# A sliding-window attention layer: probabilities rearranged through DRAM, half 1 normalized early, finishing and low parts moved

## The chip, the cores and the metric

The kernel runs on one core of a Trainium2 chip. The metric is the device time of one execution in microseconds (us); the lower, the better. The engines named below are TensorE (PE for matmuls, PEld for its weight loads), VectorE (DVE), ScalarE (ACT), GpSimd (POOL) and SyncE (SP), which here issues all the DMA transfers.

## The reference

With DEPTH = 1 only the first mixer runs: sliding-window attention with 32 query heads of 64, 4 key/value heads, a window of 128, ALiBi penalties and one learned sink per head. All of it is float32, on 1024 tokens of 2048 features.

```python
h = rmsnorm(x, g_pre)
q, k, v, z = split(h @ w_in)              # 2048, 256, 256 and 2048 columns
for each block n of 128 queries:          # keys: blocks n-1 and n
    scores = q @ k.T / 8 - slope[head] * dist          # masked to 0 <= dist < 128
    p = softmax(concat(scores, sink[head]))[..., :-1]
    o = p @ v
y = (o * silu(z)) @ w_out
out = x + rmsnorm(y, g_post)
```

## The kernel before

**Precision.** Every float32 operand of the large products is split in a high part, rounded to the matmul's type, and a low part, the remainder. Three products (high by high, low by high, high by low) are accumulated, so each product costs three matmuls of 128 x 512. ACT makes the high part by a cast, DVE the low part by a subtraction.

**Order.** The 1024 tokens are worked in two halves of 512 (four blocks of 128). Each half has, in this order: the V projection (`v_slot`, `v_evac`), the K projection (`k_phase`, `k_evac`), the attention stage `in_phase` (called in0 and in1 here) and the output stage (out0 and out1), four chunks `c` of 512 output columns. In out0 the input of half 1 is also prepared. The fourth chunk of out1 runs block by block at the very end (`acc_l`, L793), from weights kept whole in `wl`.

**The weight stream.** `stream` lists all weight granules (128 x 512) in their order of use. `pump_dma` (L187) loads the raw granule on SP's queue, `pump_split` (L200) makes its two parts and `next_granule` (L222) hands them to the matmuls, with a look-ahead of 2 splits and 5 loads, four raw buffers and nine for low parts. In half 0 the low parts of the V, K and input projections are stored to DRAM (L218) and in half 1 loaded (L196) in place of DVE's subtraction. The output weights are split again in each half. Those of out1's fourth chunk are among the granules of its second and third chunk (`wl_hi`, `wl_lo`, both L213 and L215).

**The attention stage.** `in_phase` has 8 quads of 4 heads. A quad is 16 slots; each slot is one granule and 12 matmuls of the projections of q (two accumulators) and z (two). Events (`at(slot, ...)`, run by `run_events`) put the attention's instructions between the slots: `att_scores` (matmul L312, mask, minimum, exponential L368), `att_transpose` in slot TSL = 12 of a block's own count, `att_values` in slot VSL = 15. A block of 128 queries takes four slots. `att_transpose` divides the exponentials by their sum in three DVE operations (L377), transposes 32 x 32 squares on DVE (L384), moves 16 squares of 32 x 128 to their places (L389: nine copies on ACT, four on DVE, three on POOL), splits the result (L392, L393), and has POOL cut it into the parts of the two key blocks (L397, L401). `att_values` multiplies by the values (L422) and by the gate (L437). `f` and `g`, which hold the cut probabilities, have one buffer each.

**Normalization.** The scale of a token, 1/rms, is not applied to the input. It is multiplied in where the projections leave PSUM: `v_evac` (`rhalf`), `k_evac` (L295), `q_evac` (L460), `z_evac` (L473), the last three on DVE with the row `rrow`. In out0, `prep_load` and `x_square` compute the squares of half 1 from 1 MB loads `xt` (L679, L249, L252), and `chunk_load` (L685) with `chunk_split` (L693 to L695) transposes and splits its input.

**Finishing.** The rows of half 0 lie in `y_dram` after out0 (L718). `finalize` (L559 to L564) loads them and x, scales and adds on DVE and stores the result; this runs in slots 142 to 175, in out1.

**What orders the instructions.** At build time the tile framework orders each engine's instructions by a planned timeline; an instruction in `keep_in_program_order` stays in the order of the program among those pinned. From slot 125 of a half (PIN_FROM) through the first 13 output slots (SPILL) the matmuls are pinned. An engine works strictly in its order, so a wait holds up all that follows on it; that goes for SP's queue of transfers too.

## Time and profile before

| what | value |
|---|---|
| median of 3 runs | 1314.67 us (1310.45 to 1317.33) |
| the profiled execution | 1312.46 us |
| its span, first to last instruction | 1310.4 us |
| granted clock of TensorE, mean | 0.995 |
| PE busy | 1261.4 us, 96% |
| PEld busy | 1038.2 us, 79% |
| DVE busy | 1001.3 us, 76% |
| ACT busy | 807.4 us, 62% |
| POOL busy | 302.5 us, 23% |
| moved by DMA | 225.79 MB, 172 GB/s |

Busy is the time in which an engine has at least one instruction at work. Matmuls overlap, so a PE that is busy throughout is one that is fed throughout. A share over the whole span is an average over stages that differ, so the argument goes by stages. Idle time of an engine costs something only where another engine waits for it.

### The profile page before, as it was taken

To read this page: it belongs to the slowest core of one execution; us is meant where nothing else is said; L and a number is where in the kernel's file an instruction comes from. 1 tells how busy PE (TensorE), PEld (TensorE's weight loads), DVE (VectorE), ACT (ScalarE), POOL (GpSimd) and SP (SyncE) were. 2 spreads that over 40 slices of the span, in tenths; PEclk is the share of its full clock that TensorE was granted. 3 is DMA by queue.
4 is the path that set the end of the run, shared out by engine and by line. 5 is a ranking of instruction groups with operands and counts; after the bars stand their busy time and mean duration, and the time that the engine had idled before them with its cause. 6 is when DMAs were issued, how large, how long until landed. Compare 5 with 4: busy or idle time off the path is not lost. (4 is left out here: it accounts for less than half of the span.)

```text
span 1310.4 us, 20613 instructions
## 1 busy us (share of the span) xinstructions
PE 1261.4 (96%) x5889; PEld 1038.2 (79%) x5889; DVE 1001.3 (76%) x2840; ACT 807.4 (62%) x2131; POOL 302.5 (23%) x561
## 2 busy tenths in 40 slices
PE   8999999999999998999999999999999999998897
PEld 8888777787787776778898888888888887776676
DVE  5759999989989998676722478878878878966555
ACT  4537666666676676555533477767767767644441
POOL 1303233323323323000002033333333333300000
PEclk9999999999999999999999999999999999999999
DMA  8565545455454533967686665565555552288715
GB/s 290 176 194 161 161 153 163 151 173 162 132 177 153 170 105 90 242 162 180 171 249 189 182 180 170 166 177 171 168 176 171 169 161 81 78 274 271 251 56 187
DMA packets 263793, 225.79 MB, mean 172 GB/s; under 512 B 47088, under 2 KB 195072, under 8 KB 263680
## 3 DMA queue, kind: packets, MB, share of 16 engines
q1 hardware_dynamic: 263680, 224.48, 57.2%
q8 instruction: 47, 0.77, 0.3%
q14 instruction: 66, 0.54, 0.1%
HBM read 174.09 MB, written 50.33 MB: 171 GB/s over the span
## 5 line engine op out<-in xcount | busy, mean ns | idle before, releaser
L312 PE MATMUL acc_i<-h_hi,g_lo 128*128 128x512 f32 x1024 | 403.3, 394 | 4.9 <-DVE g_lo L215 4.5
L312 PE MATMUL acc_i<-h_hi,g_hi 128*128 128x512 f32 x1024 | 402.3, 393 | 3.1 <-ACT g_hi L213 2.9
L312 PE MATMUL acc_i<-h_lo,g_hi 128*128 128x512 f32 x1024 | 400.9, 392 | 0.0
L213 ACT CAST g_hi<-raw 128x512 fp32r<-128x512 f32 x400 | 245.6, 615 | 123.5 <-PE acc_i L312 34.1
L312 PEld LDWEIGHTS acc_i<-h_hi,g_hi 128*128 128x128 f32 x1024 | 192.5, 188 | 45.9 <-ACT g_hi L213 6.7
L312 PEld LDWEIGHTS acc_i<-h_hi,g_lo 128*128 128x128 f32 x1024 | 192.6, 188 | 44.9 <-DVE g_lo L215 11.7
L312 PEld LDWEIGHTS acc_i<-h_lo,g_hi 128*128 128x128 f32 x1024 | 192.7, 188 | 38.2
L389 ACT COPY px<-wt 32x128 f32<-32x128 f32 x576 | 171.2, 297 | 67.4 <-DVE wt L384 60.8
L215 DVE TENSOR_TENSOR g_lo<-raw,g_hi 128x512 fp32r<-128x512 f32 x256 | 186.2, 728 | 27.3 <-ACT g_hi L213 18.9
L368 ACT ACTIVATE t<-t,m 128x129 f32<-128x129 f32 x256 | 102.6, 401 | 107.3 <-DVE m L358 103.8
L397 POOL TENSOR_SCALAR_AFFINE_SELECT g<-f 64x512 fp32r<-64x512 f32 x112 | 90.5, 808 | 225.2 <-ACT f L392 218.8
L523 DVE TENSOR_TENSOR u_lo<-u,u_hi 128x512 fp32r<-128x512 f32 x128 | 88.9, 697 | 44.2 <-ACT u_hi L522 44.2
L522 ACT CAST u_hi<-u 128x512 fp32r<-128x512 f32 x128 | 78.6, 617 | 62.4 <-PE acc_l L793 24.5
L312 PE MATMUL acc_o<-g_lo,u_hi 128*128 128x512 f32 x256 | 101.9, 398 | 6.6 <-DVE g_lo L215 6.6
L312 PE MATMUL acc_o<-g_hi,u_lo 128*128 128x512 f32 x256 | 100.1, 395 | 0.0
L339 POOL COPY t<-nsink 128x4 f32<-128x4 f32 x64 | 18.6, 293 | 332.0 <-DVE w L377 208.4
L401 POOL TENSOR_SCALAR_AFFINE_SELECT f<-f 64x512 fp32r<-64x512 f32 x112 | 83.7, 747 | 39.9 <-DVE f L393 25.0
L358 DVE CUSTOM_DVE_ANT_0 t<-s_ps,t,nsink 128x128 f32<-128x128 f32 x256 | 87.6, 348 | 4.6
L312 PE MATMUL acc_o<-g_hi,u_hi 128*128 128x512 f32 x256 | 85.1, 397 | 3.6 <-ACT g_hi L213 2.6
L312 PE MATMUL acc_s<-g_lo,u_hi 128*128 128x512 f32 x192 | 75.7, 395 | 7.7 <-DVE g_lo L215 7.6
L312 PE MATMUL s_ps<-k_x,q 128*128 128x320 f32 x256 | 76.6, 311 | 4.3 <-DVE s_ps L356 1.5
L389 POOL COPY px<-wt 32x128 f32<-32x128 f32 x192 | 64.5, 336 | 68.4 <-DVE wt L384 58.0
(138 smaller groups left out, 2089.7 us busy)
## 6 DMA issues: line engine op xcount, KB each, us to landing
raw<-in_w_in_a SPq DMA_DIRECT2D x288, 256.0 KB, 3.3
lo<-g_lo SPq DMA_DIRECT2D x144, 256.0 KB, 2.1
g_lo<-lo SPq DMA_DIRECT2D x144, 256.0 KB, 3.0
raw<-in_w_out_a SPq DMA_DIRECT2D x128, 256.0 KB, 3.8
xt<-in_x SPq DMA_DIRECT2D x4, 1024.0 KB, 7.5
xb<-in_x SPq DMA_DIRECT2D x64, 64.0 KB, 3.7
y_dram<-yg SPq DMA_DIRECT2D x16, 256.0 KB, 3.6
fin_y<-y_dram SPq DMA_DIRECT2D x16, 256.0 KB, 5.2
```

The costliest lines, as they stand in the source:

```text
L213: nc.scalar.copy(hi, raw)
L215: nc.vector.tensor_tensor(lo, raw, hi.bitcast(F32), op=ALU.subtract)
L312: ins = nc.tensor.matmul(*args, **kw)
L339: nc.gpsimd.tensor_copy(a["t", b][:, :, :, P : P + 1], nsink[:, i : i + 1].unsqueeze(2).unsqueeze(3).broadcast_to([P, 2, 2, 1]))
L358: nc.vector.tensor_tensor_reduce(out=t[:, 0:P], in0=s3[:, 0, QTR:], in1=t[:, 0:P], scale=1.0, scalar=nsink[:, i : i + 1], op0=ALU.add, op1 ...
L368: nc.scalar.activation(t, t, AF.Exp, bias=m, scale=-1.0, accum_out=den)
L389: copy(x[qrows[3 - k], c, :], wt[qrows[c], 3 - k, :])
L397: nc.gpsimd.affine_select(out=g[dst].rearrange("p a (s i) -> p (a s) i", i=HD), in_=part.bitcast(F32), pattern=[[0, 2 * QUAD], [-1, HD]], ...
L401: nc.gpsimd.affine_select(out=part, in_=part.bitcast(F32), pattern=[[0, 2 * QUAD], [1, HD]], compare_op=ALU.is_ge, fill=0.0, base=0, chann ...
L522: nc.scalar.copy(hi_v, src)
L523: nc.vector.tensor_tensor(lo_v, src, hi_v.bitcast(F32), op=ALU.subtract)
```

## The change

- **Probabilities.** The division by the sum goes from three DVE operations to six ACT operations (`AF.Copy` with a scale per partition). For the first seven quads of a half the 16 moves become one DMA write of the 256 KB tile to DRAM (`pd`, four buffers) and four reads of 64 KB with the squares in their places. The last quad (`fast`) keeps the 16 moves. The tag `w` gets three buffers instead of two, `att_values` slot 17 instead of 15, and the copies of the values (`v_twice`) slot 14 instead of 12.
- **Half 1 normalized in its split.** The squares of half 1 are computed in in0 on ACT, pinned, from 16 loads of 256 KB (`xp`); `chunk_split` multiplies by the row `rrow1` on DVE. In half 1 `v_evac` scales by 0.5, and `k_evac`, `q_evac` and `z_evac` read PSUM with no multiplication first. `prep_load` and the squares leave out0; `xb` gets four buffers instead of two, `xtr` two instead of one, and the loads are issued three slots earlier.
- **Finishing.** `y_scale` and the 16 `finalize` pieces of half 0 run in in1, in slots 10 to 119, seven slots apart, with the DVE operation pinned and two buffers per tile instead of four shared.
- **Low parts.** Every granule's low part made in half 0 is stored, the output weights' 64 too, and in half 1 every granule has its low part loaded; for the fourth chunk directly into `wl`. The look-ahead of splits is 3 instead of 2, with four buffers for high parts instead of three and six for low parts instead of nine.

```diff
+G_BUFS = 4
+LOOK_W = 3
-LO_BUFS = 9
+LO_BUFS = 6
+SQ_SLOT, FIN_SLOT, FIN_STEP = 12, 10, 7
+W_BUFS = 3
+PD_BUFS = 4
-SSL, TSL, VSL = 8, 12, 15
+SSL, TSL, VSL = 8, 12, 17
...
             lo = None
-            if i - first in kept:
-                lo = lo_tile()
-                nc.sync.dma_start(lo.bitcast(F32), kept[i - first])
+            if key in kept:
+                lo = wl[1][:, kind, :] if isinstance(kind, int) else lo_tile()
+                nc.sync.dma_start(lo.bitcast(F32), kept[key])
...
             nc.scalar.copy(hi, raw)
-            if isinstance(kind, int) or made:
+            if lo is None:
+                lo = lo_tile()
                 nc.vector.tensor_tensor(lo, raw, hi.bitcast(F32), op=ALU.subtract)
-            if keeps(i):
-                kept[i] = dram.tile([P, 512], F32, name=f"lo{i}")
-                nc.sync.dma_start(kept[i], lo.bitcast(F32))
+                kept[key] = dram.tile([P, 512], F32, name=f"lo{i}")
+                nc.sync.dma_start(kept[key], lo.bitcast(F32))
...
-    def k_evac(pk, t):
-        k32 = gp.tile([P, 512], F32, tag="tmp", name="k32", bufs=1)
-        nc.vector.tensor_tensor(k32, pk, rrow, op=ALU.mult)
+    def k_evac(pk, t, half):
+        k32 = pk
+        if not half:
+            k32 = gp.tile([P, 512], F32, tag="tmp", name="k32", bufs=1)
+            nc.vector.tensor_tensor(k32, pk, rrow, op=ALU.mult)
...
-    def att_transpose(a, half, b):
+    def att_transpose(a, half, b, fast):
...
-        w = pool.tile([P, QUAD, 2, 2, QTR], F32, tag="w", name="w", bufs=2)
-        for e, dst, src, n in ((0, 0, QTR, 3), (0, 3, 0, 1), (1, 0, 0, 4)):
-            nc.vector.tensor_tensor(
-                w[:, dst : dst + n, :, e, :].rearrange("p g s i -> p s g i"),
-                t[:, :, e, src : src + n * QTR].rearrange("p s (g i) -> p s g i", i=QTR),
-                rec[:, :, e : e + 1].unsqueeze(3).broadcast_to([P, 2, n, QTR]),
-                op=ALU.mult,
-            )
+        w = pool.tile([P, QUAD, 2, 2, QTR], F32, tag="w", name="w", bufs=W_BUFS)
+        for s in range(2):
+            for e, dst, src, n in ((0, 0, QTR, 3), (0, 3, 0, 1), (1, 0, 0, 4)):
+                nc.scalar.activation(
+                    w[:, dst : dst + n, s, e, :],
+                    t[:, s, e, src : src + n * QTR].rearrange("p (g i) -> p g i", i=QTR),
+                    AF.Copy, scale=rec[:, s, e : e + 1],
+                )
...
+        if fast:
+            for n in range(QUAD * QUAD):
...
+        else:
+            pd = dram.tile([P, QUAD * P], F32, tag="pd", name="pd", bufs=PD_BUFS)
+            nc.sync.dma_start(pd, wt.rearrange("p g c -> p (g c)"))
+            src = pd.rearrange("(c i) (k j) -> k i c j", i=QTR, j=P)
+            for k in range(QUAD):
+                nc.sync.dma_start(x[qrows[k]], src[k])
...
+            if half:
+                nc.scalar.mul(qh, src[here], scale)
+                nc.vector.scalar_tensor_tensor(
+                    lo, src[here], scale, qh.bitcast(F32), op0=ALU.mult, op1=ALU.subtract
+                )
+            else:
+                nc.scalar.copy(qh, src[here])
+                nc.vector.tensor_tensor(lo, src[here], qh.bitcast(F32), op=ALU.subtract)
...
+        src = acc
+        if not half:
+            nc.vector.tensor_tensor(z, acc, rrow, op=ALU.mult)
+            src = z
+        nc.scalar.activation(th, src, AF.Tanh, scale=0.5)
+        nc.vector.scalar_tensor_tensor(z, th, 1.0, src, op0=ALU.add, op1=ALU.mult)
...
     def finalize(pool, b, c):
...
-        yt = pool.tile([P, 512], F32, tag="xt1", name="fin_y", bufs=4)
-        xt = pool.tile([P, 512], F32, tag="xt1", name="fin_x", bufs=4)
+        yt = pool.tile([P, 512], F32, tag="xt1", name="fin_y", bufs=2)
+        xt = pool.tile([P, 512], F32, tag="xt1", name="fin_x", bufs=2)
...
         def finish():
-            nc.vector.scalar_tensor_tensor(yt, yt, r2[:, 0, b : b + 1], xt, op0=ALU.mult, op1=ALU.add)
+            tc.keep_in_program_order(
+                nc.vector.scalar_tensor_tensor(yt, yt, r2[:, 0, b : b + 1], xt, op0=ALU.mult, op1=ALU.add)
+            )
...
+        def sq_load(b, c):
+            xp = att.tile([P, 512], F32, tag="xp", name="xp", bufs=1)
+            nc.sync.dma_start(xp, xf[HALF + b * P : HALF + (b + 1) * P, c * 512 : (c + 1) * 512])
+            at(SQ_SLOT + 6 * (4 * b + c) + 4, lambda: sq_make(xp, b, c))
+
+        def sq_make(xp, b, c):
+            xjunk = att.tile([P, 512], BF16, tag="oc", name="xjunk", bufs=1)
+            tc.keep_in_program_order(nc.scalar.activation(xjunk, xp, AF.Square, accum_out=ssx1[:, b, c : c + 1]))
+
+        for b in range(NB):
+            for c in range(4):
+                at(SQ_SLOT + 6 * (4 * b + c), lambda b=b, c=c: sq_load(b, c))
+        at(SQ_SLOT + 6 * 16 + 4, lambda: x_scales(ssx1, rcol1))
         in_phase(0, h0, u0, att)
...
-            xt = op.tile([P, HALF], F32, tag="xtr", name="xtr", bufs=1)
+            xt = op.tile([P, HALF], F32, tag="xtr", name="xtr", bufs=2)
             tc.keep_in_program_order(nc.vector.transpose(xt, xts.pop(("b", k))))
+            nc.vector.tensor_tensor(xt, xt, rrow1, op=ALU.mult)
...
-        for c in range(4):
-            s0 = OUT_SLOT + 12 * c
-            at(s0, lambda c=c: prep_load(c))
-            at(s0 + 5, lambda c=c: x_square(xts[c], c, junks))
         for k in range(KC):
-            at(OUT_SLOT + 3 * k, lambda k=k: chunk_load(k))
+            at(OUT_SLOT + max(3 * k - 3, 0), lambda k=k: chunk_load(k))
             at(OUT_SLOT + 3 + 3 * k, lambda k=k: chunk_split(k))
-        at(191, x_scales)
...
+        for b in range(NB):
+            at(2 * b, lambda b=b: y_scale(0, b))
+            for c in range(4):
+                s0 = FIN_SLOT + FIN_STEP * (4 * b + c)
+                at(s0, lambda b=b, c=c: fin_start(b, c))
+                at(s0 + 4, lambda b=b, c=c: fins.pop((b, c))())
         in_phase(1, h1, u1, att)
```

134 lines of the change are left out of this document (58 added, 76 removed).

## The prediction

> **What bounds the kernel now.** I read the busy times by stage first, because the stages have different limits. The columns are the stretch, its length, the busy time (and instructions) of PE, PEld, DVE, ACT and POOL, the granted clock, the DMA share and GB/s.
>
> ```profile
> core 0: us, PE busy (x) PEld busy (x) DVE busy (x) ACT busy (x) POOL busy (x), PEclk, DMA share, GB/s
> 60.20:474.30 414.10, 401.25 (x1811) 323.52 (x1809) 372.42 (x1156) 273.35 (x788) 119.82 (x214) 1.00 0.54 163
> 474.30:530.80 56.50, 50.45 (x225) 40.83 (x224) 48.17 (x130) 38.23 (x100) 15.29 (x23) 0.97 0.36 103
> 530.80:578.70 47.90, 44.41 (x194) 35.80 (x193) 33.38 (x58) 26.22 (x54) 0.00 (x0) 1.00 0.80 198
> 578.70:622.20 43.50, 43.50 (x194) 36.02 (x193) 31.34 (x52) 25.73 (x51) 0.00 (x0) 1.00 0.75 185
> 622.20:665.70 43.50, 43.50 (x193) 36.02 (x192) 27.72 (x49) 24.36 (x48) 1.42 (x1) 1.00 0.72 196
> 711.00:1100.40 389.40, 389.40 (x1826) 325.58 (x1825) 299.56 (x1009) 277.00 (x794) 121.72 (x241) 1.00 0.56 167
> 1100.40:1155.00 54.60, 50.37 (x226) 41.04 (x225) 47.51 (x123) 36.62 (x95) 17.67 (x26) 0.97 0.34 112
> 1155.00:1205.90 50.90, 46.02 (x194) 35.32 (x193) 33.04 (x52) 22.56 (x45) 0.00 (x0) 1.00 0.84 277
> 1205.90:1258.10 52.20, 46.73 (x193) 34.96 (x191) 32.16 (x51) 25.14 (x53) 0.00 (x0) 1.00 0.60 197
> ```
>
> PE is the bound, and the rows say where it is not fed. In1 (711 to 1100) is the model: PE busy in every microsecond. In0 (60 to 474) does the same projections and attention with 15 fewer matmuls recorded and needs 24.7 us more; its DVE is busy 372.4 of 414.1 us (90%), against 299.6 of 389.4 (77%) in in1. An output chunk that is fully fed takes 43.5 us (third and fourth chunk of out0), a slot of 12 matmuls 43.5 / 16 = 2.72 us. The second chunk of out0 is 4.4 us over that, the second and third of out1 7.4 and 8.7 us. These four sums, 24.7 + 4.4 + 7.4 + 8.7 = 45.2 us, are what the edits can reach; both first output chunks also hold the last quad's attention.
>
> The list of waits names what PE's feeders stood for (total us, times, longest):
>
> ```profile
> DVE junk L252 <- DMA xt<-in_x: 12.0, 4, 3.7
> DVE wl_lo L215 <- ACT wl_hi L213: 21.0, 9, 3.1
> DVE fin_y L563 <- DMA fin_x<-in_x: 12.9, 8, 3.0
> ACT wl_hi L213 <- DMA raw<-in_w_out_a: 46.6, 15, 5.1
> PEld o_ps L422 <- POOL f L401: 11.0, 16, 1.9
> PE o_ps L422 <- POOL f L401: 5.6, 5, 1.7
> ```
>
> DVE stands in its own order behind the squares of half 1 in out0 and behind the finishing and the kept low parts in out1; the g_lo subtractions that PE needs queue behind them. At the attention's end (o_ps) little is lost now.
>
> **Probabilities: DVE's relief.** The prices, busy and mean ns before what they waited for:
>
> ```profile
> L377 DVE TENSOR_TENSOR w<-t,rec 128x256 f32<-128x256 f32 x64 | 28.6, 446 | 0.0
> L377 DVE TENSOR_TENSOR w<-t,rec 128x192 f32<-128x192 f32 x64 | 25.4, 397 | 1.5
> L377 DVE TENSOR_TENSOR w<-t,rec 128x64 f32<-128x64 f32 x64 | 16.2, 253 | 0.0
> L389 ACT COPY px<-wt 32x128 f32<-32x128 f32 x576 | 171.2, 297 | 67.4 <-DVE wt L384 60.8
> L389 DVE COPY px<-wt 32x128 f32<-32x128 f32 x256 | 69.4, 271 | 4.7
> L694 ACT ACTIVATE h_hi<-xtr,gcol 128x512 fp32r<-128x512 f32 x16 | 11.6, 724 | 22.7 <-DVE xtr L693 22.7
> L213 ACT CAST g_hi<-raw 128x512 fp32r<-128x512 f32 x400 | 245.6, 615 | 123.5 <-PE acc_i L312 34.1 <-issue 21.7 <-PE acc_v L575 16.2
> L460 DVE SCALAR_TENSOR_TENSOR q<-acc_i,rrow 128x256 f32<-128x256 f32 x64 | 26.8, 419 | 34.6 <-PE acc_i L312 33.6
> L473 DVE TENSOR_TENSOR z<-acc_i,rrow 128x512 f32<-128x512 f32 x32 | 22.0, 686 | 7.7 <-PE acc_i L312 7.3
> ```
>
> Each half has 32 blocks; 28 go through DRAM, the last quad's four keep the copies. The three DVE multiplies cost 446 + 397 + 253 = 1.10 us a block and leave all 32; four DVE copies (1.08 us) and nine on ACT (2.67 us) leave 28. DVE in in0 becomes 372.4 - 28 x 2.18 - 4 x 1.10 = 307 us. The six multiplies new on ACT have no row. From the cast and the copy, (615 - 297) / (512 - 128) = 0.83 ns per element and 191 ns fixed; a scale read per partition added 724 - 615 = 109 ns. For 96, 32 and 128 elements, twice: 2 x (380 + 327 + 406) = 2.23 us a block, 1.57 without the 109. I take 2.23, since the scale is such an operand. ACT in in0, with 16 squares of half 1 at a cast's 0.6 us: 273.4 - 28 x 2.67 + 32 x 2.23 + 9.8 = 280 us. So in0 would carry 307 of DVE and 280 of ACT, almost in1's loads of now (300 and 277), under which PE never waited. I take 22 of its 24.7 us as gained; bounds are 25 (all) and 0 (PE's stalls were order, not load). The squares are pinned on ACT behind their xp loads; the loads are issued four slots, some 12 us, ahead.
>
> **Probabilities: the longer path.** One block of in1 in the timeline, then what transfers took from issue to landing (the last figure of each, us; the last line is that of the raw loads from 1155 to 1258, minimum, median and maximum):
>
> ```profile
> 907.19 0.17 DVE L374 RECIPROCAL rec<-den 128x4 f32<-128x4 f32 x1
> 908.27 0.70 DVE L384 STREAM_TRANSPOSE wt<-w 128x512 f32<-128x512 f32 x1
> 909.01 2.77 ACT L389 COPY px<-wt 32x128 f32<-32x128 f32 x9 [0.60 <-DVE wt L384]
> 912.72 0.61 ACT L392 CAST f<-px 128x512 fp32r<-128x512 f32 x1
> 916.09 0.66 POOL L401 TENSOR_SCALAR_AFFINE_SELECT f<-f 64x512 fp32r<-64x512 f32 x1
> 917.51 0.28 PE L422 MATMUL o_ps<-f,v_s 128*128 128x256 f32 x1
> 840.94 0.38 SPq L192 DMA_DIRECT2D raw<-in_w_in_a  x1
> ```
>
> ```profile
> lo<-g_lo SPq DMA_DIRECT2D x144, 256.0 KB, 2.1
> xb<-in_x SPq DMA_DIRECT2D x64, 64.0 KB, 3.7
> y_dram<-yg SPq DMA_DIRECT2D x16, 256.0 KB, 3.6
> fin_y<-y_dram SPq DMA_DIRECT2D x16, 256.0 KB, 5.2
> DMA to landing us min/median/max: 3.0/5.0/6.4
> ```
>
> From the reciprocal to the end of the last select it is 916.75 - 907.19 = 9.6 us, and the code allows three slots, from TSL 12 to VSL 15: 3 x 389.4 / 128 = 9.1 us. After, the copies' 2.8 us become a write (2.1 as the lo stores), three more issues of 0.38 and a 64 KB read (3.7 as xb): 6.9 us, and the multiplies 1.1 us more: 9.6 + 4.1 + 1.1 = 14.8 us in five slots (VSL 17), 15.2 us. The ratio of path to slots is the one that hardly stalls now, so I price it at nothing in in0 (DMA share from 0.54 to about 0.68) and carry its risk as a rival. SP issues everything: per block it now has 4 raw and 4 lo transfers and gets five more, about 13 x 0.38 = 4.9 us, plus the wait for the write's landing, 2.1, in a block of 12.2 us. The raw and lo transfers queued behind that wait are late by as much, but are issued several slots ahead. POOL loses three copies a block; its selects stay.
>
> **Half 1 normalized in its split.** In out0 chunk_split gets 16 DVE multiplies of 0.69 us (11 us over three chunks); the 8 squares on DVE and 8 on ACT leave, with the waits for xt, 12.0 us. That would give the second chunk its 4.4 us. But the low parts of 64 output granules are now stored: 64 x 0.262 = 16.8 MB less 4.2 MB of xt, 3.1 MB a chunk. At the second out1 chunk's price, 0.84 x 50.9 us for 50.9 x 0.277 = 14.1 MB, that is 3.03 us of full DMA per MB, 9.5 us a chunk: 0.80 x 47.9 + 9.5 = 47.8, then 42.1 and 40.8 us against 43.5. So the transfers nearly fill the stage; I take zero for out0, bounds -4.4 and +10. In in1 32 of the q multiplies (0.42) and 16 of z (0.69) leave DVE, 24 us that PE did not wait for: nothing.
>
> **Finishing moved into in1.** Sixteen times two loads, a pinned DVE operation and a store leave out1: 48 x 0.262 = 12.6 MB, 38 us of DMA, 0.10 of in1's share; with the probabilities' 14.7 MB (0.11) it goes from 0.56 to 0.77. If a load is later than its four slots (12 us), DVE stands with g_lo-free work behind it: the scores and attention, for which PE then waits. Landings of 5.2 us fit. For pins, SP's queue and the higher share I take +4 us in in1, bounds 0 and, in the rival, 63.
>
> **Low parts kept.** Out1 loses 64 DVE subtractions, and the wl_lo waits (21.0 us) with them; its second and third chunk each load 24 granules twice, 48 x 0.262 + 0.26 = 12.8 MB. At the highest rate shown for it, 277 GB/s, this takes 46.4 us; the floor is 43.5. I take 46.4, a gain of 50.9 + 52.2 - 92.8 = 10.3 us; bounds 16 and 0. The raw ring of four turns once per landing plus cast, 5.0 + 0.6 us, 24 x 5.6 / 4 = 34 us, which is no bound.
>
> **First chunks.** The last quad keeps its copies but takes its multiplies from DVE to ACT, 1.1 us longer in a pinned order: 0 to 4.4 us a half, I take 1 each.
>
> The sum is -22 + 0 + 4 - 10.3 + 2 = -26 us. The profiled execution took 1312.5 us (span 1310.4); the median shown is 2.2 us above it. From the median: **1288 us**, its own range 1272 to 1304.
>
> **Rivals.** (1) The DRAM path arrives late in in1. For it: the share nears the 0.84 at which raw loads took 5.0 us, and SP waits in line. If the write lands like y_dram (3.6) and the reads like fin_y (5.2), the path is 3.0 us longer; 0.76 us of that is covered (916.75 to 917.51), and 2.24 x 28 = 63 us stall PE: 1351 us. It decides from 26 / 28 = 0.9 us a block. Against: the first matmul of o_ps is not pinned, and today's path, as tight, cost 16.6 us in all. Chance 0.20. The Trainium skill ("DMA: Bandwidth & Descriptors", Latency and other measured facts) says an HBM access goes from 0.2 us on average to 2 us at high load; by it two hops grow by an estimated 3.6 us, and this rival would be some 80 us of stall. No run here shows that yet.
> (2) DMA fills both output stages: no use above a 0.9 share makes out0's three chunks 53, 47 and 45 us, 10 over now, and out1's gain of 10 is lost: 1308. For it the 47.8 us above, against it 277 GB/s at 0.84. Chance 0.14.
> (3) The edit moves DVE's work but not PE's: the in0 stalls were the order of single instructions. 1310. For it: in0's DVE is not full, 90%. Against: in1. Chance 0.10.
> (4) All stages reach their floors: -25 - 4.4 - 16 = 1269. Chance 0.20.
> The forecast has 0.36.
>
> **How the numbers follow.** A measurement of this kernel tells about 0.5% (6.6 us) from no change. Faster is the forecast, (4) and 0.10 of (2): 0.66; same is the rest of (2) and most of (3): 0.13; slower is (1) and 0.01 of (3): 0.21. The range reaches to (4)'s side and half way into (1): 1260 to 1325.
>
> **What would show it.** In0 near 392 us with DVE near 80% busy; in1 still with PE busy throughout; o_ps waits no larger than 17 us; out1's second and third chunk at 44 to 48 us without DVE waits. A total of o_ps waits of 30 us or more, or SP standing for pd, would prove me wrong.

## The result and the profile after

The changed kernel takes 1350.68 us (median of 4, 1341.90 to 1355.99) where the kernel before, run beside it, takes 1313.45 (median of 4). The ratio is 1.0275, 95% interval 1.0212 to 1.0339: slower by 37 us, where 26 us of gain were forecast. The profiled execution is the slowest of the four, 1355.99 us with a span of 1354.3; stages are compared with the profiled execution of before (span 1310.4), 43.9 us shorter.

The stretches of the changed kernel, cut like those of before at the first and last matmuls of a stage's accumulators: the time up to the first input projection, in0, the four chunks of out0, in1, the first three chunks of out1. Columns as in the table of before.

```profile
core 0: us, PE busy (x) PEld busy (x) DVE busy (x) ACT busy (x) POOL busy (x), PEclk, DMA share, GB/s
0.00:66.40 66.40, 57.55 (x365) 52.91 (x366) 39.88 (x78) 31.44 (x59) 14.58 (x36) 1.00 0.71 228
66.40:488.20 421.80, 399.14 (x1810) 322.99 (x1809) 325.58 (x972) 257.23 (x750) 96.68 (x131) 0.99 0.66 204
488.20:539.30 51.10, 48.94 (x229) 40.32 (x228) 43.38 (x108) 40.95 (x112) 14.91 (x23) 1.00 0.59 171
539.30:583.00 43.70, 43.70 (x194) 36.22 (x193) 32.38 (x52) 24.27 (x46) 0.00 (x0) 1.00 1.01 275
583.00:626.50 43.50, 43.50 (x193) 36.02 (x193) 33.46 (x54) 23.97 (x46) 0.00 (x0) 1.00 0.92 255
626.50:669.90 43.40, 43.40 (x193) 35.92 (x193) 30.02 (x49) 23.50 (x46) 0.00 (x0) 1.00 0.83 257
714.70:1155.20 440.50, 406.34 (x1824) 330.39 (x1823) 227.56 (x775) 241.38 (x713) 101.72 (x156) 0.98 0.71 213
1155.20:1211.30 56.10, 51.89 (x227) 42.46 (x226) 34.14 (x98) 40.25 (x112) 16.68 (x26) 0.94 0.74 249
1211.30:1255.30 44.00, 44.00 (x194) 35.90 (x193) 12.96 (x19) 23.55 (x47) 0.00 (x0) 1.00 0.74 252
1255.30:1301.70 46.40, 45.17 (x194) 35.46 (x193) 15.54 (x23) 25.01 (x51) 0.00 (x0) 1.00 0.54 180
```

In1 is 51 us longer, although DVE carries 72 us less there and ACT 36 us less. The output stages did what was hoped, and more: their chunks run at the floor or close to it. In0 shed 47 us of DVE work and is still 7.7 us longer. The first stretch is 6.2 us longer (60.2 before). So PE is no longer starved by a busy engine; something idle keeps it waiting. The list of waits over the whole span (total us, times, longest):

```profile
POOL g L401 <- ACT f L396: 393.1, 49, 13.4
ACT f L396 <- DMA px<-pd: 172.2, 53, 8.8
DVE f L397 <- ACT f L396: 153.4, 51, 8.0
PEld o_ps L426 <- POOL f L405: 82.5, 75, 4.7
PE o_ps L426 <- POOL f L405: 54.0, 50, 4.3
```

ACT's cast of the probabilities (`f`, L396) stands for the reads `px` in nearly every one of the 56 blocks that go through DRAM. DVE's subtraction behind it stands with it, and at the end the matmuls of `o_ps` stand for the cut `f`. Before, ACT's cast did not wait for a transfer, and DVE's subtraction stood 12.7 us in all for the cast. (POOL's wait in the first line was 218.8 us before; POOL has time to spare.) ACT's and DVE's waits in in1 alone:

```profile
ACT f L396 <- DMA px<-pd: 127.2, 28, 8.8
DVE f L397 <- ACT f L396: 122.3, 28, 8.0
```

That is 127.2 / 28 = 4.5 us a block. The timeline of one block of in1 (start, duration, engine, line; in brackets the idle time before it and its releaser):

```profile
921.53 0.17 DVE L371 RECIPROCAL rec<-den 128x4 f32<-128x4 f32 x1
921.73 1.65 ACT L375 ACTIVATE w<-t,rec 128x96 f32<-128x96 f32 x6 [0.45 <-DVE rec L371]
923.41 0.71 DVE L381 STREAM_TRANSPOSE wt<-w 128x512 f32<-128x512 f32 x1 [0.88 <-ACT w L375]
924.39 0.46 SPq L390 DMA_DIRECT2D pd<-wt  x1
926.81 0.40 ACT L365 ACTIVATE t<-t,m 128x129 f32<-128x129 f32 x1
927.71 1.74 SPq L393 DMA_DIRECT2D px<-pd  x4
930.70 0.31 PE L309 MATMUL s_ps<-k_x,q 128*128 128x320 f32 x1
931.10 0.62 ACT L396 CAST f<-px 128x512 fp32r<-128x512 f32 x1 [3.79 <-DMA px<-pd]
931.75 0.69 DVE L397 TENSOR_TENSOR f<-px,f 128x512 fp32r<-128x512 f32 x1 [4.08 <-ACT f L396]
933.33 0.23 DVE L353 COPY_PREDICATED s_ps<-mask,s_ps 128x64 f32<-128x64 uint32 x1
934.61 0.66 POOL L405 TENSOR_SCALAR_AFFINE_SELECT f<-f 64x512 fp32r<-64x512 f32 x1
934.79 0.40 ACT L365 ACTIVATE t<-t,m 128x129 f32<-128x129 f32 x1 [2.06 <-DVE m L355]
935.31 0.18 DVE L371 RECIPROCAL rec<-den 128x4 f32<-128x4 f32 x1 [0.56 <-ACT t L365]
```

The path of this block is no longer than forecast. From the end of the transpose (924.12) to the cast (931.10) it takes 7.0 us, forecast 6.9; from the reciprocal to the end of the last select 935.27 - 921.53 = 13.7 us, forecast 14.8. It is one of the shortest: over in1's 28 blocks that go through DRAM the path takes 15.2 us on the mean (13.6 to 18.8), 0.4 more than forecast. What was not forecast is who waits inside it. ACT is idle for 3.79 us before the cast and has the next block's last exponential behind it. DVE is idle for 4.08 us before the subtraction and has the mask of the next block's scores (L353) behind it: the scores are there at 931.0 (s_ps), their mask starts at 933.33. So the next reciprocal comes 935.31 - 921.53 = 13.8 us after this one, in a block that PE can do in 389.4 / 32 = 12.2. Each block's path now begins only when the path of the block before has ended on ACT and DVE. Over in1 the reciprocals are 14.2 us apart on the mean, against 12.3 before; 28 times the difference of 1.85 us is 52 us, the 51 by which in1 is longer.

### The profile page after: what moved, and what is told of

Same layout as the page of the kernel before. It is cut to its first block, busy times and chain, and to the rows that moved or that the text cites. A ratio compares the mean times of both kernels' runs of the same rounds, so it can differ in the third digit from the quotient of the medians.

```text
span 1354.3 us, 20502 instructions
## 1 busy us (share of the span) xinstructions
PE 1272.1 (94%) x5889; PEld 1045.4 (77%) x5889; DVE 829.8 (61%) x2309; ACT 756.5 (56%) x2027; POOL 255.8 (19%) x393
## 5 line engine op out<-in xcount | busy, mean ns | idle before, releaser
L309 PE MATMUL acc_i<-h_hi,g_lo 128*128 128x512 f32 x1024 | 402.7, 393 | 0.0
L401 POOL TENSOR_SCALAR_AFFINE_SELECT g<-f 64x512 fp32r<-64x512 f32 x112 | 102.5, 915 | 451.7 <-ACT f L396 393.1
L212 DVE TENSOR_TENSOR g_lo<-raw,g_hi 128x512 fp32r<-128x512 f32 x208 | 148.6, 715 | 36.1 <-ACT g_hi L209 33.8
L397 DVE TENSOR_TENSOR f<-px,f 128x512 fp32r<-128x512 f32 x64 | 45.2, 707 | 153.6 <-ACT f L396 153.4
L396 ACT CAST f<-px 128x512 fp32r<-128x512 f32 x64 | 39.7, 620 | 172.6 <-DMA px<-pd 172.2
L375 ACT ACTIVATE w<-t,rec 128x96 f32<-128x96 f32 (+2 forms) x384 | 105.7, 353 | 11.5 <-DVE rec L371 10.9
L309 PE MATMUL acc_o<-g_hi,u_hi 128*128 128x512 f32 x256 | 101.5, 397 | 3.4 <-DVE z L491 2.2
L426 PE MATMUL o_ps<-f,v_s 128*128 128x256 f32 x128 | 44.4, 353 | 57.7 <-POOL f L405 54.0
L426 PEld LDWEIGHTS o_ps<-f,v_s 128*128 128x128 f32 x128 | 24.6, 192 | 88.1 <-POOL f L405 82.5
L405 POOL TENSOR_SCALAR_AFFINE_SELECT f<-f 64x512 fp32r<-64x512 f32 x112 | 87.8, 785 | 12.0 <-DVE f L397 3.7
```

The lines of the kernel that those rows point to most:

```text
L212: nc.vector.tensor_tensor(lo, raw, hi.bitcast(F32), op=ALU.subtract)
L309: ins = nc.tensor.matmul(*args, **kw)
L375: nc.scalar.activation(w[:, dst : dst + n, s, e, :], t[:, s, e, src : src + n * QTR].rearrange("p (g i) -> p g i", i=QTR), AF.Copy, scale= ...
L397: nc.vector.tensor_tensor(f[:, 1], x, f[:, 0].bitcast(F32), op=ALU.subtract)
L401: nc.gpsimd.affine_select(out=g[dst].rearrange("p a (s i) -> p (a s) i", i=HD), in_=part.bitcast(F32), pattern=[[0, 2 * QUAD], [-1, HD]], ...
L405: nc.gpsimd.affine_select(out=part, in_=part.bitcast(F32), pattern=[[0, 2 * QUAD], [1, HD]], compare_op=ALU.is_ge, fill=0.0, base=0, chann ...
```

## The experiments

Stage lengths, read from the stretches of each kernel's profiled execution, with the ratio of the times to the kernel before. "Rest" of out0 is its second to fourth chunk; c1, c2, c3 are out1's first three chunks, c3 up to the fourth chunk's first matmul. Diffs are against the changed kernel unless they say otherwise.

| kernel | start | in0 | out0 c1 | rest | in1 | out1 c1 | c2 | c3 | ratio [95%] |
|---|---|---|---|---|---|---|---|---|---|
| before | 60.2 | 414.0 | 56.6 | 134.9 | 389.2 | 54.8 | 50.9 | 52.3 | 1 |
| after | 66.4 | 421.8 | 51.1 | 130.6 | 440.6 | 56.1 | 44.0 | 46.4 | 1.0275 [1.0212, 1.0339] |
| e1_moves | 65.2 | 422.6 | 56.0 | 130.6 | 398.7 | 56.0 | 44.8 | 46.1 | 1.0037 [1.0017, 1.0057] |
| e2_pin | 65.6 | 402.9 | 58.9 | 130.6 | 416.8 | 53.1 | 43.5 | 46.0 | 1.0017 [0.9999, 1.0034] |
| e3_vsl | 66.6 | 415.4 | 66.8 | 130.6 | 415.4 | 58.4 | 44.3 | 45.5 | 1.0208 [1.0180, 1.0237] |
| e4_fins | 66.8 | 419.5 | 52.7 | 130.6 | 420.6 | 56.0 | 43.5 | 44.1 | 1.0121 [1.0089, 1.0153] |
| e5_wdve | 65.2 | 435.1 | 54.1 | 130.6 | 423.7 | 54.5 | 44.1 | 47.9 | 1.0315 [1.0266, 1.0364] |
| e6_grow | 60.3 | 417.7 | 51.1 | 130.6 | 434.7 | 54.4 | 44.0 | 47.0 | 1.0178 [1.0141, 1.0215] |
| e7_noprob | 66.1 | 416.1 | 56.5 | 130.6 | 388.7 | 50.4 | 45.1 | 45.0 | 0.9869 [0.9836, 0.9903] |
| e8_prob | 61.6 | 413.7 | 51.7 | 138.7 | 411.8 | 55.6 | 53.8 | 52.3 | 1.0154 [1.0114, 1.0193] |
| e9_mix | 60.5 | 402.7 | 59.2 | 130.6 | 388.7 | 50.6 | 46.4 | 46.1 | 0.9779 [0.9755, 0.9803] |
| e10_pin_fins_grow | 60.6 | 402.2 | 59.3 | 130.6 | 387.3 | 54.0 | 43.5 | 44.9 | 0.9729 [0.9696, 0.9762] |
| e11_unpin | 65.5 | 418.3 | 52.7 | 130.6 | 447.1 | 53.2 | 43.5 | 46.9 | 1.0400 [1.0366, 1.0435] |
| e12_rest_grow | 59.1 | 414.0 | 58.1 | 130.6 | 388.7 | 52.0 | 44.8 | 45.9 | 0.9829 [0.9806, 0.9853] |
| e13_finq | 60.9 | 409.2 | 56.9 | 130.6 | 410.1 | 56.1 | 44.4 | 47.2 | 0.9941 [0.9921, 0.9962] |
| e14_slot | 60.7 | 420.1 | 55.2 | 130.6 | 421.9 | 57.9 | 43.5 | 44.2 | 1.0107 [1.0060, 1.0154] |
| e15_cast | 60.1 | 405.0 | 53.0 | 130.6 | 388.3 | 51.0 | 43.6 | 45.3 | 0.9722 [0.9688, 0.9755] |
| e16_q6 | 63.0 | 410.6 | 53.1 | 130.6 | 387.4 | 50.7 | 43.9 | 45.2 | 0.9743 [0.9713, 0.9772] |
| e17_half0 | 60.6 | 388.5 | 53.0 | 130.6 | 388.4 | 53.7 | 43.5 | 43.5 | 0.9595 [0.9577, 0.9613] |
| e18_sq | 60.0 | 400.7 | 51.1 | 131.1 | 389.2 | 52.1 | 43.5 | 45.6 | 0.9705 [0.9685, 0.9726] |

### Which part of the change costs the time

**The moves on the engines again, the rest of the change kept:**

```diff
-        if fast:
+        if True:
```

> The changed kernel with the 16 moves in all quads, no probabilities through DRAM; the rest of the change stays (att_values in slot 17, multiplies on ACT, finishing in in1). Theory A (the DRAM path is late and ACT, DVE and POOL stand in order behind its f cast): in1 falls from 441 to about 391 us, in0 from 422 to about 392, the total from 1351 to about 1271. Theory B (the pinned finishing and its transfers disturb in1): in1 stays above 425 us and the total above 1310. Theory C (the multiplies on ACT lengthen the path): o_ps waits stay above 80 us and the total above 1310.

Without the way through DRAM in1 falls to 398.7 us, 42 less; in0 stays at 422.6, where theory A expected about 392. So most of in1's loss hangs on the DRAM way, that of in0 does not hang on it alone: here ACT carries the division and the nine copies.

**The change without the part of the probabilities** (the division on DVE, the 16 moves, the slots and the two buffers of `w` of before):

```diff
-SSL, TSL, VSL = 8, 12, 17
+SSL, TSL, VSL = 8, 12, 15
...
-        for s in range(2):
-            for e, dst, src, n in ((0, 0, QTR, 3), (0, 3, 0, 1), (1, 0, 0, 4)):
-                nc.scalar.activation(
+        for e, dst, src, n in ((0, 0, QTR, 3), (0, 3, 0, 1), (1, 0, 0, 4)):
+            nc.vector.tensor_tensor(
...
-        if fast:
+        if True:
```

> The change without all of its part on the probabilities: division on DVE, the 16 moves, att_values in slot 15, the copies of the values in slot 12, two buffers w. Theory A with C: in0 about 400 us (before 414: DVE has the same work as before there, so little is gained), in1 about 392, the total about 1285. Theory E (in0 loses by the pinned squares or the look-ahead, in1 by the pinned finishing): in0 stays above 412 and in1 above 400 us, the total above 1300.

Faster than before by 1.3%: in1 at PE's floor, with the finishing in it, and the output stages at theirs.

**The kernel before with this part alone** (the division on ACT, `pd`, VSL 17, three buffers for `w`, `v_twice` in slot 14):

```diff
-SSL, TSL, VSL = 8, 12, 15
+SSL, TSL, VSL = 8, 12, 17
...
+        if fast:
...
+            pd = dram.tile([P, QUAD * P], F32, tag="pd", name="pd", bufs=PD_BUFS)
+            nc.sync.dma_start(pd, wt.rearrange("p g c -> p (g c)"))
...
```

> The kernel before with the part on the probabilities alone (division on ACT, the way through DRAM for seven quads, att_values in slot 17, three buffers w). Theory A with C: in0 about 420 us and in1 about 415, since PE stalls at o_ps in both; the total about 1345. Theory E: in0 falls to about 395, in1 stays about 392, the total about 1295.

Slower by 1.5%. In0 and in1 of this kernel:

```profile
61.60:475.30 413.70, 397.80 (x1811) 323.94 (x1810) 326.09 (x965) 246.21 (x716) 96.02 (x130) 0.99 0.64 199
711.00:1122.80 411.80, 399.50 (x1824) 323.58 (x1823) 241.14 (x816) 248.50 (x716) 108.27 (x157) 1.00 0.63 195
```

DVE has 46 us less to do in in0 than before (372.4) and the stage is as long as before; in1 is 22 us longer. The parts do not add: this one alone +20 us, the rest alone -17, together +37. Something else in the change makes the DRAM way dearer.

**The division back on DVE**, the DRAM way kept (the three DVE multiplies in place of the six on ACT):

```diff
-                nc.scalar.activation(
-                    w[:, dst : dst + n, s, e, :],
...
+            nc.vector.tensor_tensor(
+                w[:, dst : dst + n, :, e, :].rearrange("p g s i -> p s g i"),
```

> The changed kernel with the division by the sum back on DVE, in three operations; the way through DRAM stays. Theory C (the six multiplies on ACT are half of the loss: they hold up the next exponentials and the casts behind them): in0 falls from 422 to about 400 us, in1 from 441 to about 420, the total to about 1310. Theory A alone (only the DRAM path is late): in0 and in1 within 6 us of the changed kernel, the total 1345 to 1355.

In0 is 13 us longer, in1 17 shorter (423.7, near what theory C expected), and the total (1354.76) can't be told from the changed kernel's. So the division on ACT has a part in in1's loss beside the rest of the change, but does not explain it: 34 of the 51 us stay.

### What of the DRAM way: the price of the transfers or the place of the cast

**Two slots more for the path:**

```diff
-SSL, TSL, VSL = 8, 12, 17
+SSL, TSL, VSL = 8, 12, 19
...
-                at(s0 + 14, lambda y=y, kv=i // 2: y.update(t=v_twice(pool, kv)))
+                at(s0 + 16, lambda y=y, kv=i // 2: y.update(t=v_twice(pool, kv)))
```

> The changed kernel with att_values in slot 19 instead of 17 and the copies of the values in slot 16; nothing pinned. Theory D: PE has 6 us more work before it needs a block, so its o_ps waits nearly vanish, in1 about 395 and in0 about 395 us, the total about 1285. Theory A: ACT still stands about 170 us for px, the scores behind it stay late, in1 stays above 410 us and the total above 1305.

In1 415.4, in0 415.4, and ACT's `f` still stands for `px` 106.7 us in in1. More room for the matmuls of `o_ps` does not free ACT and DVE: PE's waits at `o_ps` in in1 fall from 31.0 us to 1.5, but PE now stands 13.3 us at the next scores (`s_ps`) for DVE's `q` (1.5 in the changed kernel).

**The split as an event of its own, four slots after the transpose, with the cast pinned there:**

```diff
-SSL, TSL, VSL = 8, 12, 17
+SSL, TSL, VSL = 8, 12, 18
+FSL = 16
...
+    def att_split(a, half, b, pin):
...
-        nc.scalar.copy(f[:, 0], x)
+        ins = nc.scalar.copy(f[:, 0], x)
+        if pin:
+            tc.keep_in_program_order(ins)
...
+                at(sb + (TSL_LAST if last else FSL), lambda a=a, b=b, last=last: att_split(a, half, b, not last))
```

> The changed kernel with the DRAM path, but the f cast and what follows are an event of their own in slot 16, the f cast pinned on ACT behind all that is traced before it; att_values in slot 18 instead of 17, the copies of the values in slot 15. Theory A: ACT no longer stands for px (172 us now, under 50 then), the exponentials of the next block are no longer late, in1 falls to about 400 us and in0 to about 400, the total to about 1290. Theory D (the path is simply longer than the slots allow, wherever ACT's cast stands): one slot more than now gives back 3 us of 2.9 per block at the most half the time, in1 about 420, the total about 1325.

In0 loses 19 us, in1 24 of its 51; the time is that of the kernel before. Right in direction, and not all: ACT's wait for `px` in in1 is 95.5 us.

**The finishing back in out1** (not pinned, four shared buffers, as before):

```diff
-                s0 = FIN_SLOT + FIN_STEP * (4 * b + c)
-                at(s0, lambda b=b, c=c: fin_start(b, c))
-                at(s0 + 4, lambda b=b, c=c: fins.pop((b, c))())
...
+                s0 = OUT_SLOT + 1 + 2 * (4 * b + c)
+                at(s0, lambda b=b, c=c: fin_start(b, c))
+                at(s0 + 3, lambda b=b, c=c: fins.pop((b, c))())
```

> The changed kernel with the finishing of half 0 back in out1, in its old slots and buffers and not pinned. Theory A: in1 keeps most of its loss and stays above 425 us, out1 goes back up by 5 to 10 us, the total stays about 1350. Theory B: in1 falls to about 395 us and the total to about 1315.

In1 420.6, 20 less (between the figures of theories A and B), with out1 no longer than in the changed kernel. So the finishing is most of what makes the DRAM way dearer than in e8_prob (20 of 440.6 - 411.8 = 29 us in in1), though it costs nothing beside the moves on the engines (e7_noprob).

**Cast moved, finishing in out1, and `grow` loaded at once (e6_grow below):** e2_pin with e4_fins and e6_grow.

```diff
+FSL = 16
...
+                s0 = OUT_SLOT + 1 + 2 * (4 * b + c)
...
+        grow = rrow[0:KC, 0:P]
```

> Both halves through DRAM with the f cast pinned in slot 16 and att_values in slot 18, the finishing back in out1, the tile grow free at once. Theory A with the finishing as its aggravation: in1 falls from 417 us (with the finishing in it) to about 400, out1's second and third chunk rise by 2 us each at most, the total about 1300. If the finishing plays no part once the cast is pinned, in1 stays at 415 and the total at 1311.

1279.32 us, 2.7% faster than before, in1 at PE's floor with the whole DRAM way in it. The two edits taken apart, both with the finishing in out1 and `grow` loaded at once: only the values one slot later (VSL 18, `v_twice` 15, the cast not touched),

```diff
-SSL, TSL, VSL = 8, 12, 17
+SSL, TSL, VSL = 8, 12, 18
```

> As the run with the cast pinned and the finishing in out1, but nothing split off or pinned on ACT: only att_values one slot later (18) and the copies of the values in slot 15. Theory A (ACT's early cast holds up the next exponentials): ACT stands over 60 us for px in in1, in1 stays at 410 us or more, the total about 1305 or more. Theory D (PE asked a slot too early): in1 about 390, the total about 1282.

and only the cast's event (cast, subtraction and selects in slot 16, the cast pinned), with the values in slot 17 as in the changed kernel:

```diff
 SSL, TSL, VSL = 8, 12, 17
+FSL = 16
```

> As the run with the cast pinned and the finishing in out1, but att_values back in slot 17 (copies of the values in 14): only the pinned f cast in slot 16. Theory A: the exponentials are in time, but PE asks for a block one slot (3 us) earlier than in that run, where 6 us lay between the low parts and o_ps and some 4 us of that are the selects: in1 about 390 to 395, the total about 1287. Theory D: in1 stays at 415 or more, the total 1308 or more.

In1 of e14_slot, the stretch, then ACT's and DVE's waits in it and PE's two longest:

```profile
711.30:1133.20 421.90, 396.76 (x1824) 326.88 (x1824) 214.97 (x760) 237.25 (x711) 102.59 (x156) 0.99 0.64 193
```

```profile
ACT f L396 <- DMA px<-pd: 116.1, 27, 5.9
DVE f L397 <- ACT f L396: 100.0, 28, 5.5
PE s_ps L309 <- DVE q L476: 13.3, 7, 2.8
PE o_ps L426 <- POOL f L405: 9.0, 12, 1.4
```

The same of e15_cast: in1, ACT's and DVE's waits in it, then one block:

```profile
693.40:1081.70 388.30, 388.30 (x1825) 325.40 (x1823) 221.10 (x765) 247.67 (x716) 101.88 (x157) 1.00 0.72 212
```

```profile
DVE f L404 <- ACT f L401: 20.5, 20, 2.1
ACT f L401 <- DMA px<-pd: 19.8, 19, 1.9
```

```profile
901.46 0.18 DVE L372 RECIPROCAL rec<-den 128x4 f32<-128x4 f32 x1
910.30 0.23 DVE L354 COPY_PREDICATED s_ps<-mask,s_ps 128x64 f32<-128x64 uint32 x1 [0.80 <-PE s_ps L310]
911.34 0.62 ACT L401 CAST f<-px 128x512 fp32r<-128x512 f32 x1 [0.30 <-DMA px<-pd]
911.99 0.69 DVE L404 TENSOR_TENSOR f<-px,f 128x512 fp32r<-128x512 f32 x1 [0.30 <-ACT f L401]
913.63 0.18 DVE L372 RECIPROCAL rec<-den 128x4 f32<-128x4 f32 x1
914.73 0.66 POOL L412 TENSOR_SCALAR_AFFINE_SELECT f<-f 64x512 fp32r<-64x512 f32 x1
```

This settles in1 as long as the finishing is in out1. The path of the block is as long as in the changed kernel's block, 915.39 - 901.46 = 13.9 us against 13.7. But the next block's mask (910.30) now stands ahead of the subtraction (911.99), ACT waits 0.30 us instead of 3.79, and reciprocals are 12.2 us apart instead of 13.8. In e14_slot the values had a slot more and the cast stayed: no gain, and PE's waits at `o_ps` are small (9.0 us) while it stands for DVE's `q`. The cleanest pair is e14_slot and e10_pin_fins_grow, which differ in the cast's event alone: in1 421.9 and 387.3 us, in0 420.1 and 402.2. (That the event was moved and that it was pinned were not tried one without the other.)

**In half 0 one slot later still:** e15_cast with the cast in slot 17, values 18 and `v_twice` 15 of half 0; half 1 as in e15_cast.

```diff
-                at(sb + (TSL_LAST if last else FSL), lambda a=a, b=b, last=last: att_split(a, half, b, not last))
+                at(sb + (TSL_LAST if last else FSL + 1 - half), lambda a=a, b=b, last=last: att_split(a, half, b, not last))
...
-                    sb + (VSL_LAST[b] if last else VSL),
+                    sb + (VSL_LAST[b] if last else VSL + 1 - half),
```

> The run with only the cast pinned (finishing in out1, grow free at once, 1279 us), with half 0 alone one slot later: f cast in 17, att_values in 18, copies of the values in 15. In that run ACT still stands 36.6 us for px in in0 and in0 takes 405 us. If that is the same cause still at work: ACT's waits for px under 15 us in in0, in0 about 395, the total about 1270. If in0's rest comes from elsewhere (the division of DVE and ACT between lo, squares and scores): in0 stays at 400 or more.

1261.73 us, 4.0% faster than before (ratio 0.9595, 0.9577 to 0.9613): the fastest here. In0 of it, then its waits in in0:

```profile
60.60:449.20 388.60, 387.03 (x1811) 323.81 (x1810) 320.85 (x970) 256.06 (x746) 83.43 (x131) 1.00 0.72 222
```

```profile
ACT f L401 <- DMA px<-pd: 0.7, 2, 0.5
```

The same wait in in0 of e15_cast:

```profile
ACT f L401 <- DMA px<-pd: 36.6, 23, 3.8
```

ACT's wait goes from 36.6 us to 0.7, and in0 loses 16.5 us. In e10_pin_fins_grow, with the values in slot 18 and the cast still in 16, in0 was 402.2; so most of the gain, 13.7 us, is the cast's slot.

### The smaller terms

**`grow` not in the released memory of the prologue** (the 8 KB tile of `g_pre`, which the change had moved from the pool `const` to the pool `pro`; here it gets a part of `rrow`, in `const`):

```diff
-        grow = pro.tile([KC, P], F32, name="grow")
+        grow = rrow[0:KC, 0:P]
```

> The changed kernel with the small tile grow (g_pre as rows) in memory that no earlier DVE work uses, so that its load is issued at once. The prologue up to the first projection of in0 takes 60 us as before instead of 66; the total is 6 us shorter, about 1345. If the prologue's loss has another cause, it stays at 66 us.

The start is 60.3 us again, 6.1 less. The timeline after, and that of before, at this load:

```profile
4.89 0.60 DVE L110 SCALAR_TENSOR_TENSOR distb<-maskf,distb 128x32 f32<-128x32 f32 x1
5.58 0.35 SPq L618 DMA_DIRECT2D grow<-in_g_pre  x1
11.91 0.26 PE L624 MATMUL gps<-ident,grow 16*128 16x16 f32 x1 [2.12 <-DMA grow<-in_g_pre]
```

```profile
1.29 0.49 SPq L599 DMA_DIRECT2D grow<-in_g_pre  x1
3.95 0.28 PE L605 MATMUL gps<-ident,grow 16*128 16x16 f32 x1
```

The load is issued 4.3 us later, just after DVE's last use of `maskf`; PE's first use moves from 3.95 to 11.91. That `grow` got `maskf`'s memory fits the times; the edit shows only that its new place is the cause. The rest of this run's gain over the changed kernel lies in in0 and in1 and is within the spread of the changed kernel's own times.

**The rest of the change, with `grow` loaded at once:** e7_noprob with e6_grow.

```diff
-        if fast:
+        if True:
...
+        grow = rrow[0:KC, 0:P]
```

> The change without its part on the probabilities and with the tile grow free at once: prologue 60 us instead of 66, the rest as in the run without the probabilities' part; the total about 1292, ratio to before about 0.982.

1291.78. In1, with the finishing in it and the moves on the engines, is at PE's floor: 388.7 us, PE busy throughout. In0 is as long as before, 414.0.

**Half 0 through DRAM with the cast moved, half 1 with the division on DVE, the moves on the engines and the finishing in in1:**

```diff
-        if fast:
+        if fast or half:
...
+                at(sb + (TSL_LAST if last else TSL if half else FSL), lambda a=a, b=b, last=last: att_split(a, half, b, not last and not half))
...
+                    sb + (VSL_LAST[b] if last else 15 if half else VSL),
```

> Half 0 with the way through DRAM, the f cast pinned in slot 16 and att_values in slot 18; half 1 with the division on DVE, the 16 moves and slot 15; the rest of the change as it is, the tile grow free at once. If the relief of DVE pays in in0 once ACT no longer stands early for px: in0 about 403 us, in1 about 389, prologue 60, the total about 1280 and about 12 below the next kernel but one of this call. If not, in0 is 414 or more and the total 1291 or more.

1284.96: 7 us better than e12_rest_grow (in0 11 us shorter), and 23 us short of e17_half0, of which 14 in in0.

**What the finishing does to the DRAM way.** Not pinned, in the changed kernel:

```diff
-            tc.keep_in_program_order(
-                nc.vector.scalar_tensor_tensor(yt, yt, r2[:, 0, b : b + 1], xt, op0=ALU.mult, op1=ALU.add)
-            )
+            nc.vector.scalar_tensor_tensor(yt, yt, r2[:, 0, b : b + 1], xt, op0=ALU.mult, op1=ALU.add)
```

> The changed kernel with the finishing in in1 but its DVE operations not pinned. If the pin is what makes the finishing cost 20 us in in1: in1 about 421, the total about 1331. If it is the transfers and SP's queue: in1 stays about 440 and the total about 1351.

Worse: in1 447.1, with DVE standing 47.5 us (9 times) for `fin_x` in it. On ACT's queue of transfers instead of SP's, in e2_pin with e6_grow:

```diff
-        nc.sync.dma_start(yt, y_dram[rows, cols])
+        nc.scalar.dma_start(yt, y_dram[rows, cols])
...
-            nc.sync.dma_start(of[rows, cols], yt)
+            nc.scalar.dma_start(of[rows, cols], yt)
```

> Cast pinned in slot 16, att_values in slot 18, finishing in in1, the tile grow free at once; the finishing's loads and stores are issued on ACT's queue instead of SP's. If SP's order (the probabilities' transfers wait in line behind a finishing load that waits for a store) makes the 29 us by which in1 is longer with the finishing: in1 about 392, the total about 1282. If it is the transfers themselves (longer landings) or DVE: in1 about 415, the total about 1310.

In1 410.1, against 416.8 in e2_pin on SP's queue and 387.3 without the finishing. ACT's `f` stands for `px` 63.8 us (95.5 in e2_pin, 5.3 in e10_pin_fins_grow). So neither the pin nor SP's queue is the whole reason. The transfers themselves are longer. The table has the hop, from the end of a block's transpose to the landing of its last read, over in1's 28 blocks (worked out from each run's timeline), and the time between reciprocals:

| kernel | finishing | cast | hop, mean (shortest to longest) us | reciprocals, mean us | in1 us |
|---|---|---|---|---|---|
| after | in1 | slot 12 | 8.2 (5.7 to 12.1) | 14.2 | 440.6 |
| e4_fins | out1 | slot 12 | 7.4 (6.5 to 8.7) | 13.5 | 420.6 |
| e14_slot | out1 | slot 12 | 7.3 (5.7 to 8.3) | 13.6 | 421.9 |
| e2_pin | in1 | slot 16 | 8.5 (5.6 to 13.1) | 13.3 | 416.8 |
| e13_finq | in1, ACT's queue | slot 16 | 8.3 (5.7 to 12.6) | 13.1 | 410.1 |
| e10_pin_fins_grow | out1 | slot 16 | 6.9 (5.9 to 8.7) | 12.2 | 387.3 |
| e15_cast | out1 | slot 16 | 7.1 (5.4 to 8.6) | 12.3 | 388.3 |

From the reciprocal to the end of the transpose it is another 2.8 us in e2_pin and 3.0 in e10_pin_fins_grow. So, as an estimate, the last read lands 2.8 + 8.5 = 11.3 us after the reciprocal in the first and 9.9 in the second. In both the cast's event stands four slots, 10.9 us, behind the transpose's: behind the landing in the second, ahead of it in the first. In the changed kernel the 16 hops with a transfer of the finishing issued beside them (or up to 2 us before) take 8.9 us on the mean, the other 12 take 7.3. In e11_unpin the hop is 7.4 us and DVE stands for `fin_x` instead. Why the transfers land later beside the finishing's, no run here shows. The table also parts the two causes: e14_slot and e10_pin_fins_grow have nearly the same hop, and in1 differs by 35 us.

**Two that moved little.** The seventh quad's values a slot earlier, in e10_pin_fins_grow:

```diff
-                    sb + (VSL_LAST[b] if last else VSL),
+                    sb + (VSL_LAST[b] if last else VSL - (i == NQUAD - 2)),
```

> The fastest run so far (cast pinned in 16, att_values in 18, finishing in out1, grow free at once) with the seventh quad's att_values in slot 17, so that its z buffers are free earlier for the last quad. The two first output chunks shorten by about 5 us in half 0 and 2 in half 1, the total about 1273; if the last quad's z does not wait for them, no change, 1279.

1281.40 against 1279.32, intervals overlapping, out0's first chunk 6 us shorter and in0 8 us longer: the time moves from one stage to the other. The squares of half 1 not pinned, in e15_cast:

```diff
-            tc.keep_in_program_order(nc.scalar.activation(xjunk, xp, AF.Square, accum_out=ssx1[:, b, c : c + 1]))
+            nc.scalar.activation(xjunk, xp, AF.Square, accum_out=ssx1[:, b, c : c + 1])
```

> The same run with the 16 squares of half 1 in in0 not pinned on ACT. If the pins make ACT wait in order for the loads xp or move the exponentials behind the cast: in0 falls from 405 to about 395 us, the total to about 1270. If not: in0 403 to 407, the total about 1279.

1275.95 against 1279.18, intervals overlapping; in0 is 400.7 us against 405.0, between the two figures expected. What the pin of the squares costs can't be told from nothing here.

## Why the prediction was wrong, step by step

**The step that failed** is "I price it at nothing in in0 ... and carry its risk as a rival", said of the longer path; in1's term of the sum, +4, holds nothing for it either. In1 became 51 us longer, in0 7.8. The length of the path was about right: 14.8 us forecast, 15.2 measured on the mean of in1's blocks (14.3 with the finishing in out1, e4_fins). Its terms over the whole kernel:

```profile
L375 ACT ACTIVATE w<-t,rec 128x96 f32<-128x96 f32 (+2 forms) x384 | 105.7, 353 | 11.5 <-DVE rec L371 10.9
```

```profile
pd<-wt SPq DMA_DIRECT2D x56, 256.0 KB, 3.4
px<-pd SPq DMA_DIRECT2D x224, 64.0 KB, 2.2
```

The six multiplies took 105.7 / 64 = 1.65 us a block (forecast 2.23); the write landed in 3.4 us (2.1), the reads in 2.2 (3.7). The comparison that the path was put into was wrong. "The ratio of path to slots is the one that hardly stalls now" sets the path against the slot of the last consumer, `o_ps`. The first consumer is the cast on ACT, in order with the next block's exponentials, and the subtraction on DVE, in order with the next block's masks. Before, ACT filled this time with nine copies of the same path; after, with a wait: 127.2 us on ACT in in1, and 122.3 on DVE behind it. For this path the prediction named what is queued behind the wait on SP, and not what is queued behind it on ACT and DVE. Shown by e14_slot (the path given a slot more, the cast left: in1 421.9) against e10_pin_fins_grow, which differs from it in the cast's event alone (387.3).

**Rival (1)** has the time, 1351, but that is a coincidence. It put the whole price on late landings, a write like `y_dram` and reads like `fin_y`, 3.6 + 5.2 = 8.8 us where 3.4 + 2.2 = 5.6 came, and on PE at `o_ps`; ACT and DVE, which stood, are not in it. It is right in part: in1's hop took 8.2 us on the mean against 6.9 forecast, 1.3 us later and not 3.0, and 0.8 us of that goes with the finishing (e4_fins). The rule of the Trainium skill that stands beside it ("DMA: Bandwidth & Descriptors", Latency and other measured facts: an HBM access goes from 0.2 us on average to 2 us at high load) would have added an estimated 3.6 us to the hop. At a DMA share of 0.71 the mean hop was 1.3 us over the sum made from rows of before, the longest 5.2 over; how much of that is the latency that the rule means, no run here shows.

**In0, -22:** measured +7.8 in the changed kernel and -25.5 in e17_half0 (388.5 against 414.0). The reading (in0 short of DVE time, in1 as the model) was right, and so was the gain; the same cast hid it, ACT standing 44.9 us for `px` in in0. The loads were forecast less well: DVE 307 us where 325.6 came (320.9 in e17_half0), ACT 280 where 257.2 came. Only 29 of the 32 blocks lie in in0's stretch; DVE's multiplies and copies took 27.1 + 29.9 = 57 us there, not the 65 that the sum takes off. Rival (3), that the relief moves DVE's work and not PE's, looks right in e8_prob and is refuted by e17_half0, since the rest of the change alone leaves in0 at 414.0 (e12_rest_grow).

**In1, +4 for the finishing:** it is -0.5 us beside the moves on the engines (e7_noprob, 388.7) and +20 beside the DRAM way (e4_fins against after). The term was added up as if the edits were independent; they meet in the hop, which is longer beside the finishing, and in ACT's wait for `px` (95.5 us in e2_pin, 5.3 in e10_pin_fins_grow).

**Out0, 0 with a bound of -4.4:** the second chunk gained 4.2 us. Rival (2) is refuted: the DMA share of the three chunks went to 1.01, 0.92 and 0.83, that is 44.1, 40.0 and 36.0 us of DMA where 47.8, 42.1 and 40.8 had been computed, and PE was fed in every microsecond. **Low parts, -10.3:** -12.8 measured, -16.2 in e17_half0, both chunks at the floor of 43.5 us. I had set 12.8 MB a chunk against 277 GB/s; but the transfers did not keep to their chunks: 44.0 x 0.252 = 11.1 MB and 46.4 x 0.180 = 8.4 MB moved in these two, and 56.1 x 0.249 = 14.0 MB in the first, so the rate was no bound. The finishing's move gave out1 nothing: with it back there (e4_fins) the two chunks are 43.5 and 44.1 us. **First chunks, +2:** -5.5 and +1.3.

**Missing from the sum: +6.2 us in the prologue.** The move of `grow` into another pool is part of the change, though not of the lines of it shown above, and the prediction has no term for it.

**Rival (4)**, all stages at their floors, 1269, had in0 -25, out0 -4.4 and out1 -16. With the cast moved, the finishing back in out1 and `grow` loaded at once, e17_half0 shows -25.5, -4.3 and -16.2. So the gains that the sum counted were there; the place of one instruction in its engine's order hid them. The sign that the prediction set, "a total of o_ps waits of 30 us or more", came: 54.0 us on PE and 82.5 on its weight loads.

## What to carry to other kernels

When work moves from an engine to a transfer, price the path and then ask which engine holds its first consumer, and what stands behind that instruction in the engine's order: the wait is paid by all of it, and more slots for the last consumer did not help here. Put the first consumer (with its event, or by a pin) behind the landing in its engine's order, as late as the path needs; here four slots were worth 35 us of in1, and in in0 one slot more, 2.7 us, another 14. Look at the longest landings too, not only the median: the finishing cost nothing beside the moves and 20 to 30 us beside the DRAM way. A tile that changes its pool is an edit with a price too: here its load came 4.3 us later, which fits a wait for the last reader of the memory that it got.

## What was unexpected

- The DMA share reached 1.01 at 275 GB/s in out0's second chunk with PE fed throughout. A share near one was no sign of a stage bound by its transfers: at 0.84 and 277 GB/s out1's second chunk in the kernel before had been 7.4 us over the floor.
- In most stages where PE stalled often in short pieces, the granted clock was lower: in in1 0.98 after, in e2_pin and in e4_fins, 0.97 in e11_unpin, 0.99 in e14_slot, 1.00 in e15_cast and e17_half0, where it did not stall; but also 1.00 in e8_prob, where it did. PE's own busy time in in1 was 406.3 us after against 388.3 in e15_cast for nearly the same number of matmuls (1824 and 1825), so 18 of the 52 us between these two lie inside PE's busy time and not in idle time. 2% of 406 is 8 us; what makes up the other 10 (e8_prob has 399.5 us busy at a clock of 1.00), and whether stalls lower the clock, no run here separates.
